# The gate/up accumulator tile U2 gets a second buffer

## The chip, the cores and the metric

The kernel runs on one core of a Trainium2 chip. The metric is device microseconds of one execution; the time before is the median of three runs. The profile is of one further execution, whose own time is given beside its span. TensorE (PE) multiplies; ScalarE (ACT), VectorE (DVE) and GpSimd (POOL) do the elementwise work; SyncE (SP) issues the DMAs.

## The reference

One layer of an encoder over x of 1024 rows and 1024 columns, in float32: a half-step feed-forward (FFN), an attention mixer of two head groups, a second half-step FFN. The change touches the FFNs alone:

```python
f = _swiglu(_rmsnorm(x, ffn1_pre_g[l]), ffn1_w_gate[l], ffn1_w_up[l], ffn1_w_down[l])
x = x + 0.5 * _rmsnorm(f, ffn1_post_g[l])
# _swiglu: (silu(x @ w_gate) * (x @ w_up)) @ w_down, with w_gate, w_up 1024 x 2816, w_down 2816 x 1024
```

## The kernel before

Each float32 operand of a matmul is split into a high and a low part, and three matmuls (high-high, high-low, low-high; PASSES) stand for one. The split of a weight tile is a ScalarE conversion (line 117) and a subtraction on GpSimd or VectorE (line 118), into a tile wgu of a pool of five.

The class Ffn runs each half-step. The 2816 hidden columns are cut into NF = 22 blocks of 128. Block 0 is done plainly. In blocks 1 to 21 (the loop over `self.items`, method `run`), the gate and up products of the block are done together by a seven-product scheme in the manner of Strassen and Winograd, in place of eight quarter products. Rows of activations are halved, the contraction is halved, and the 128 gate and 128 up columns are taken 64 at a time. Each product is 12 matmuls of 128x128 by 512 columns. Their order in a block is P1, P6, P2, P7, P5, P4, P3 (ORDER); the last block has P1, P6, P7, P2, P4, P5, P3 (LAST).

The products go to four PSUM banks: P1 and P2 to pa, P6 to pb, P7 and P4 to pc, P5 and P3 to pd. P2 is added by TensorE onto P1 in pa. P1 alone is needed too: after P1, line 409 copies it out of pa on ScalarE into the SBUF tile U2. VectorE adds P6 to U2 (line 411), makes U3 = U2 + P7 (414) and adds P5 to it (417), makes C21 = U2 + P4 (423), and last adds P3 to U2 itself (426). The function `glu` turns two such sums into half of a hidden tile h: silu of the gate half on ScalarE (line 445), times the up half on VectorE (line 446). It runs after P2 (from pa), P5 (from U3), P4 (from C21) and P3 (from U2). So U2 of a block is read for the last time by the multiply of line 446 after P3, while P1 and P6 of the next block run. Each of U2, U3 and C21 has one buffer in the pool u. In the profile all of them are named U or C.

While a block is multiplied, the weights of the next are made. `feed` calls `prepare` for the tiles some products ahead: it loads raw gate and up columns (line 180; the tile rawgu has three buffers), combines them on GpSimd (lines 213, 214, 223, 225) and splits them. After odd blocks, `keep` stores the h tiles of a pair in DRAM for the down projection (line 333), makes three differences and a sum of them on VectorE one by one (line 337) and stores these (line 338).

The engines have one queue each and take their instructions in the order of that queue. The framework's planner sets the order before the run by planned times and by the order of the code; `issue_after` holds an instruction behind another. So an instruction may stand earlier or later on its engine than the code has it: in the rows below, a conversion of line 117 often stands ahead of a silu that the code has first. The framework also adds the waits: a tile with one buffer may be written again only once its last reader is done.

Of the kernel before, what the change touches and what calls it, by code (L numbers as in the profile page):

```python
# [10 lines left out]
F32 = mybir.dt.float32  # L11
# [25 lines left out]
def tile_macaron_block(ctx, tc, x, f1_pre, f1_post, f1_g, f1_u, f1_d, mix_pre, mix_post, w_qkv,  # L37
# [13 lines left out]
    def open_pool(name, **kw):  # L51
        kw.setdefault("bufs", 1)
        return tc.alloc_tile_pool(name=name, reuse_waits="tile", **kw)
# [66 lines left out]
    class Ffn:  # L120
# [273 lines left out]

        def gate_up(self, i, prod, ps, y, psd):
            def U(name):
                return self.u.tile([128, 4, 128], F32, name=name)

            tt, add, s = DVE.tensor_tensor, OP.add, self.S
            n = (self.ORDER if i < NF - 1 else self.LAST).index(prod)  # L400
            if i == 1 and 0 < n < 5:
                self.turn_combo(("T2", "T3", "T1", "T4")[n - 1], y, psd)
            p = self.bank(i, ps, self.BANK[prod])
            first = prod in ("P1", "P6", "P7", "P5")
            name = {"P1": "B11", "P6": "T2", "P7": "T3", "P5": "T1", "P2": "B21", "P4": "T4", "P3": "B22"}[prod]
            self.product(p, self.W[i, prod], name, first)
            if prod == "P1":
                s["u2"], s["c21"] = U("U2"), U("C21")
                ACT.activation(s["u2"], p, AF.Copy)  # L409
            elif prod == "P6":  # L410
                tt(s["u2"], s["u2"], p, op=add)
            elif prod == "P7":
                s["u3"] = U("U3")
                tt(s["u3"], s["u2"], p, op=add)
            elif prod == "P5":
                s["h1"] = self.new_h(i, 1)
                tt(s["u3"], s["u3"], p, op=add)  # L417
                self.glu(s["h1"][64:128], s["u3"], s["c21"])
            elif prod == "P2":
                s["h0"] = self.new_h(i, 0)  # L420
                self.glu(s["h0"][0:64], p, s["h0"])
            elif prod == "P4":
                tt(s["c21"], s["u2"], p, op=add)
                self.glu(s["h0"][64:128], s["c21"], s["h0"])
            elif prod == "P3":
                tt(s["u2"], s["u2"], p, op=add)
                self.glu(s["h1"][0:64], s["u2"], s["c21"])
            if i == NF - 1 and n == 3:
                self.close_tx(2)
                self.raw.release()  # L430
                self.load_left(self.AHEAD)
                self.open_down()
            if n == 6 and i % 2 == 1 and i < NF - 1:
                self.keep(i // 2)
            if n == 6 and i >= NF - 2:
                for half in range(2):
                    SP.dma_start(self.hd["h", i, half], self.H[i][half])
            if n == 6 and i == NF - 1:
                self.close_tx(1)
                self.u.release()  # L440
                self.us = open_pool("us" + self.tag, side=self.near)
                self.U = self.us.tile([128, 4, 512], F32, name="U")
# [694 lines left out]
```

## Time and profile before

| what | value |
|---|---|
| median of three runs | 2077.77 us (2077.45 to 2078.15) |
| the profiled execution | 2079.25 us, span 2077.5 us |
| PE busy | 1983.2 us (95%) |
| DVE, ACT, POOL busy | 1333.0, 1005.9, 1048.3 us |
| granted PE clock, mean | 0.990 of full speed |
| the copies of line 409 start | from 55.5 to 469.4 us (first half-step) and from 1410.8 to 1824.6 us (second) |

Times in the rows are microseconds from the start of the span unless marked ns. A row of the timeline gives the start, the busy time, the engine, the line, the operation, output and inputs with their sizes, how many instructions are merged (x), and in brackets the idle time of the engine before it and what ended it. SPq is SyncE's queue of DMA issues, PEld the loading of weights. A wait for several semaphores is put down to the one that came last by the profile.

### The profile page before, as it was taken

What the parts mean: (1) busy time and instruction counts of PE and PEld (TensorE: products, weight loads), DVE (VectorE), ACT (ScalarE), POOL (GpSimd) and SP (SyncE); (2) the same over time, 40 slices, a digit from 0 to 9 for tenths busy, and PEclk for the clock granted to TensorE, in tenths of its full rate; (3) what the DMA queues carried; (4) which work ended last, traced back from release to release, by engine and by line L of the source; (5) the groups of instructions that cost most, each with busy time, mean ns of one, the idle gap of its engine ahead of it and who ended that gap; (6) DMA issues with size and microseconds to landing.
All of it is one profiled execution on the core that took longest, in us unless ns stands there. A gap on an engine that the chain in (4) does not pass through costs nothing. (4 is left out here: it accounts for less than half of the span.)

```text
span 2077.5 us, 30443 instructions
## 1 busy us (share of the span) xinstructions
PE 1983.2 (95%) x10728; PEld 1676.4 (81%) x10728; DVE 1333.0 (64%) x2255; ACT 1005.9 (48%) x1892; POOL 1048.3 (50%) x894
## 2 busy tenths in 40 slices
PE   7999999999999799999999999999999999999996
PEld 6777777777888699998999998887777777778884
DVE  7545544547668855766999888356545444576688
ACT  5433333334444433436999999234333333344443
POOL 4555656565050614233777887315565655651504
PEclk9999999999999899999999999999999999999998
DMA  4232322326533543233040643222323232365434
GB/s 147 75 98 87 116 92 87 112 87 228 177 117 95 199 130 101 67 102 77 2 138 1 207 137 90 102 77 71 100 78 125 79 101 84 115 221 170 127 97 172
DMA packets 210681, 233.01 MB, mean 112 GB/s; under 512 B 21088, under 2 KB 147040, under 8 KB 210400
## 3 DMA queue, kind: packets, MB, share of 16 engines
q1 hardware_dynamic: 210528, 231.06, 35.3%
q8 instruction: 85, 1.39, 0.3%
q14 instruction: 68, 0.56, 0.1%
HBM read 164.95 MB, written 66.06 MB: 111 GB/s over the span
## 5 line engine op out<-in xcount | busy, mean ns | idle before, releaser
L118 POOL TENSOR_TENSOR wgu<-rawgu,wgu 128x512 fp32r<-128x512 f32 x216 | 306.8, 1428 | 385.4 <-ACT wgu L117 358.8
L117 ACT ACTIVATE wgu<-rawgu 128x512 fp32r<-128x512 f32 x302 | 181.7, 627 | 368.0 <-POOL rawgu L225 190.5
L288 PE MATMUL pa<-actT,wgu 128*128 128x512 f32 (+1 forms) x1080 | 270.4, 398 | 29.7 <-ACT U L409 28.8
L356 PE MATMUL pd<-wgu 128*128 128x512 f32 x1140 | 272.4, 390 | 3.5 <-DVE wgu L118 3.2
L288 PEld LDWEIGHTS pa<-actT,wgu 128*128 128x128 f32 x1080 | 198.6, 190 | 89.2 <-ACT U L409 44.5
L356 PEld LDWEIGHTS pd<-wgu 128*128 128x128 f32 x1140 | 213.0, 188 | 52.5 <-DVE wgu L118 6.7
L567 PE MATMUL pq<-wq,actT 128*128 128x256 f32 x1728 | 217.7, 284 | 0.7 <-ACT actT L107 0.7
L567 PEld LDWEIGHTS pq<-wq,actT 128*128 128x128 f32 x1728 | 208.9, 190 | 1.3 <-ACT actT L107 1.0
L117 ACT ACTIVATE wgu<-b 128x512 fp32r<-128x512 f32 x148 | 93.0, 631 | 204.7 <-PE pd L356 114.8
L118 DVE TENSOR_TENSOR wgu<-b,wgu 128x512 fp32r<-128x512 f32 x144 | 120.3, 837 | 103.8 <-ACT wgu L117 103.4
L767 POOL TENSOR_SCALAR P<-P,il 128x1024 f32<-128x1024 f32 (+1 forms) x128 | 130.6, 1020 | 64.3 <-DVE il L766 61.1
L446 DVE TENSOR_TENSOR h<-h,C 64x512 f32<-64x512 f32 x42 | 51.5, 1226 | 156.9 <-ACT h L445 156.9
L868 DVE TENSOR_TENSOR PT<-pt,PT 128x512 fp32r<-128x512 f32 (+1 forms) x256 | 146.2, 612 | 2.0 <-ACT PT L867 2.0
L288 PE MATMUL pd<-actT,wgu 128*128 128x512 f32 x552 | 136.2, 395 | 0.0
L288 PE MATMUL pc<-actT,wgu 128*128 128x512 f32 x552 | 136.0, 394 | 0.0
L867 ACT ACTIVATE PT<-pt 128x512 fp32r<-128x512 f32 (+1 forms) x256 | 125.4, 544 | 10.5 <-PE pt L864 7.1
L864 PE MATMUL pt<-identr,P 128*128 128x128 f32 x896 | 125.0, 275 | 1.7 <-ACT vst L702 1.1
L288 PEld LDWEIGHTS pd<-actT,wgu 128*128 128x128 f32 x552 | 103.3, 187 | 25.7 <-DVE U L417 0.6
L288 PEld LDWEIGHTS pc<-actT,wgu 128*128 128x128 f32 x552 | 103.3, 187 | 25.0 <-DVE actT L108 0.4
L288 PE MATMUL pb<-tx,wgu 128*128 128x512 f32 x504 | 122.3, 391 | 0.0
L288 PE MATMUL pc<-tx,wgu 128*128 128x512 f32 x504 | 122.3, 391 | 0.0
L288 PE MATMUL pd<-tx,wgu 128*128 128x512 f32 x504 | 121.3, 389 | 0.0
(190 smaller groups left out, 3898.9 us busy)
## 6 DMA issues: line engine op xcount, KB each, us to landing
hd<-h SPq DMA_DIRECT2D x140, 256.0 KB, 2.9
h<-hd SPq DMA_DIRECT2D x140, 256.0 KB, 2.9
rawgu<-in_ffn_w_gate_dram SPq DMA_DIRECT2D x88, 256.0 KB, 3.0
rawgu<-in_ffn_w_up_dram SPq DMA_DIRECT2D x88, 256.0 KB, 3.7
b<-in_ffn_w_down_dram SPq DMA_DIRECT2D x88, 256.0 KB, 3.4
bkT<-kd SPq DMA_DIRECT2D x32, 320.0 KB, 7.3
rawq<-in_w_qkv_dram SPq DMA_DIRECT2D x16, 512.0 KB, 4.7
bV<-vd SPq DMA_DIRECT2D x8, 640.0 KB, 4.4
```

The costliest lines, as they stand in the source:

```text
L117: ACT.activation(hi, raw, AF.Copy)
L118: return eng.tensor_tensor(lo, raw, f32(hi), op=OP.subtract).ins
L288: PE.matmul(p[:, c0:c1, :], w[:, a, k, :], self.rhs(name, b, k)[:, c0:c1, :], start=(first and n == 0), stop=(n == 11), skip_group_check=True)
L356: PE.matmul(p, A[:, a, 128 * i:128 * i + 128], B[:, b, :], start=(first and start and n == 0), stop=(end and n == 2), skip_group_check=True)
L446: DVE.tensor_tensor(dst, s[64:128], c[64:128], op=OP.mult)
L567: PE.matmul(p, actT[:, a, T, k, :], WQ[j][:, b, k, :], start=(n == 0), stop=(n == 23))
L767: POOL.tensor_scalar(P[:, 0:w], P[:, 0:w], il, 1.0, op0=OP.mult, op1=OP.mult)
L864: PE.transpose(out=p[:, j, :], in_=col(P, b0 + j), identity=ident)
L867: ACT.activation(hv, p[:, 0:n, :], AF.Copy)
L868: DVE.tensor_tensor(lv, p[:, 0:n, :], f32(hv), op=OP.subtract)
```

## The change

The inner function U of `gate_up` makes the tiles U2, C21 and U3. U2 gets two buffers, so that those of successive blocks lie in different places; C21 and U3 keep one. The pool grows by 2 KB in each partition.

```diff
         def gate_up(self, i, prod, ps, y, psd):
             def U(name):
-                return self.u.tile([128, 4, 128], F32, name=name)
+                return self.u.tile([128, 4, 128], F32, name=name, bufs=2 if name == "U2" else 1)
```

## Rows read from the trace of the kernel before

**Rows 1.** The page: TensorE's busy time, share of the span, instructions

```profile
PE 1983.2 (95%) x10728; PEld 1676.4 (81%) x10728; DVE 1333.0 (64%) x2255; ACT 1005.9 (48%) x1892; POOL 1048.3 (50%) x894
```

**Rows 2.** Waits of PE, 105.2-451.5 and 1459.9-1807: us in all, times, longest

```profile
PE pa L288 <- ACT U L409: 12.7, 18, 1.0
...
PE pa L288 <- ACT U L409: 12.3, 18, 0.7
```

**Rows 3.** The timeline of one block: TensorE's products, and one load of weights

```profile
105.39 2.62 PEld L288 LDWEIGHTS pa<-actT,wgu 128*128 128x128 f32 x12 [1.10 <-ACT U L409]
105.40 3.06 PE L288 MATMUL pa<-actT,wgu 128*128 128x512 f32 x12 [0.68 <-ACT U L409]
108.29 2.90 PE L288 MATMUL pc<-tx,wgu 128*128 128x512 f32 x12
111.02 2.88 PE L288 MATMUL pd<-tx,wgu 128*128 128x512 f32 x12
...
119.33 2.96 PE L288 MATMUL pa<-actT,wgu 128*128 128x512 f32 x12
122.14 2.90 PE L288 MATMUL pb<-tx,wgu 128*128 128x512 f32 x12
125.72 2.59 PE L288 MATMUL pa<-actT,wgu 128*128 128x512 f32 x10 [0.69 <-ACT U L409]
```

**Rows 4.** The timeline of the same block: the other engines, from P2 on

```profile
108.49 0.59 ACT L445 ACTIVATE h<-pa 64x512 f32<-64x512 f32 x1 [2.11 <-PE pa L288]
...
111.06 1.29 POOL L213 TENSOR_TENSOR rawgu<-rawgu 128x512 f32<-128x512 f32 x1
...
113.75 1.16 ACT L117 ACTIVATE wgu<-rawgu 128x512 fp32r<-128x512 f32 x2 [4.02 <-POOL rawgu L214]
...
120.25 0.63 ACT L117 ACTIVATE wgu<-rawgu 128x512 fp32r<-128x512 f32 x1 [4.69 <-POOL rawgu L225]
120.91 0.63 ACT L445 ACTIVATE h<-C 64x512 f32<-64x512 f32 x1
120.96 1.30 POOL L118 TENSOR_TENSOR wgu<-rawgu,wgu 128x512 fp32r<-128x512 f32 x1 [0.74 <-ACT wgu L117]
...
121.58 1.23 DVE L446 TENSOR_TENSOR h<-h,C 64x512 f32<-64x512 f32 x1 [4.15 <-ACT h L445]
...
122.84 0.69 DVE L426 TENSOR_TENSOR U<-U,pd 128x512 f32<-128x512 f32 x1
...
123.62 0.63 ACT L445 ACTIVATE C<-U 64x512 f32<-64x512 f32 x1 [1.42 <-DVE U L426]
...
124.29 0.69 DVE L446 TENSOR_TENSOR h<-C,U 64x512 f32<-64x512 f32 x1 [0.16 <-ACT C L445]
...
125.07 0.60 ACT L409 ACTIVATE U<-pa 128x512 f32<-128x512 f32 x1 [0.81 <-PE pb L288]
125.56 1.14 ACT L117 ACTIVATE wgu<-rawgu 128x512 fp32r<-128x512 f32 x2
```

**Rows 5.** The timeline just after, where a pair of h tiles is stored

```profile
125.01 3.12 DVE L337 TENSOR_TENSOR h<-h 128x512 f32<-128x512 f32 x3
...
126.12 0.45 SPq L180 DMA_DIRECT2D rawgu<-in_ffn_w_up_dram  x1
126.26 1.31 POOL L118 TENSOR_TENSOR wgu<-rawgu,wgu 128x512 fp32r<-128x512 f32 x1 [4.00 <-ACT wgu L117]
```

**Rows 6.** The page's DMA issues: KB each, median us from issue to landing

```profile
rawgu<-in_ffn_w_up_dram SPq DMA_DIRECT2D x88, 256.0 KB, 3.7
```

**Rows 7.** The timeline around the copy of block 2

```profile
83.80 1.54 PE L288 MATMUL pb<-tx,wgu 128*128 128x512 f32 x6
...
84.16 0.60 ACT L409 ACTIVATE U<-pa 128x512 f32<-128x512 f32 x1 [0.81 <-DVE h L446]
```

**Rows 8.** Line 409: what ended ScalarE's idle time before it (us, times)

```profile
  PE pb L288: 28.5, 35
  DVE h L446: 4.1, 5
```

## The prediction

> **What bounds the kernel now.** The page comes first: TensorE is busy 1983.2 of the 2077.5 us [rows 1], so a change that touches no matmul can win only where TensorE stands still. The waits of TensorE come next, over the two stretches in which the gate/up blocks 3 to 20 of either half-step run: there it waits for one thing alone, the copy of U2 out of pa on line 409, 18 times in each stretch and 12.7 + 12.3 = 25.0 us in all, 0.69 us a block [rows 2]. The product behind the copy is P2: it adds into the bank pa that holds P1, so it may not start before the copy has read pa.
>
> Then one block is read in order of time. From the start of one P2 to that of the next: 125.72 - 105.40 = 20.32 us [rows 3]. TensorE alone would need less. P7, P5, P4, P3 and the next P1 take 122.14 - 108.29 = 13.85; P6, with nothing to wait for, takes what the first P7 took, 111.02 - 108.29 = 2.73; a P2 that doesn't restart takes what P1 took, 122.14 - 119.33 = 2.81. Sum 19.39 us. So 0.93 us a block is lost to the copy: 0.69 of idleness, some 0.16 by which TensorE stands before it shows as idle, and 0.08 because P2 after a stop took 108.29 - 105.40 = 2.89.
>
> Why is the copy late? Follow it back [rows 4]. P2 ends, ScalarE takes silu of it (108.49), then its conversions release GpSimd (111.06), GpSimd releases ScalarE (113.75, idle 4.02 until then), GpSimd's two combinations end, the conversion at 120.25 waits 4.69 for the last of them, silu of P4 is queued behind it (120.91), VectorE multiplies (121.58), adds P3 to U2 (122.84), ScalarE takes silu (123.62), VectorE multiplies (124.29), ScalarE copies (125.07), the next P2 starts (125.72). Each waits for the one before it, from one P2 to the next. This ring, 20.32 us long, sets the period; TensorE with its 19.39 does not.
>
> **The change.** It removes one link of the ring. The multiply at 124.29 reads the old U2; with one buffer the copy may not write the new one before it is done. The copy starts 125.07 - 124.29 = 0.78 us after the multiply starts. With a second buffer it no longer needs it: P1 has ended (P6 started at 122.14, behind it), and the buffer it then gets was last read one block, some 20 us, earlier. What is left ahead of the copy is the queue of ScalarE: the silu at 123.62 stands directly before it and lasts to 124.25. So the copy starts at 124.25 plus the gap between two ScalarE instructions. No row has this pair without a wait between. Bounds: the pair of conversions at 125.56 started 0.11 before the copy ended at 125.67; the conversion at 120.25 ended at 120.88, and the silu followed 0.03 later; the copy now starts 0.09 after the multiply has ended. From -0.11 to +0.09, then; I take 0.03, another ScalarE pair on SBUF. The copy starts at 124.28 or so, 0.78 to 0.79 earlier than now; by the bounds 0.73 to 0.93.
>
> What is late next: the copy, 0.60 long, ends at 124.88, P2 starts 0.05 behind it as now (125.72 after 125.67), at 124.93. TensorE alone would be ready at 122.14 + 2.73 = 124.87. So the ring still sets the period, by a hair: 20.32 - 0.78 = 19.54 us against 19.39 of TensorE. More than 0.93 a block can't be won however early the copy is.
>
> What else moves: ScalarE's two conversions behind the copy (125.56) and GpSimd's subtraction behind them (126.26) [rows 5] come 0.78 earlier; the weights they make are used some products later. VectorE's add of P6 into U2 follows the copy, but P6 itself ends only at about 125.0, so it starts then or, after pair blocks, behind the three h differences. The second buffer costs 2 KB a partition and no instruction. No matmul, DMA, or queue position is asked for by the diff. Blocks 1, 2 and 21 win nothing: in block 2 the copy was at 84.16 while P6 was still running from 83.80 on, and P2 followed without a wait [rows 7]; in block 21 P7 stands between P6 and P2. After the half-step all work follows, shifted, as it depends on it.
>
> Sum: 36 blocks x 0.78 = 28.1 us; by the bounds 36 x 0.73 = 26.3 to 36 x 0.93 = 33.5. The profiled execution took 2079.25 us (span 2077.5): 2051.2 after. The median of the runs, 2077.77, is 1.5 below the profiled one, and the gain is the same for both: **2049.7 us**.
>
> [...] In the rows the weight load of P2 waits for the copy with the matmul (105.39, idle 1.10 against 0.68 of the matmul), and P2 then takes 2.89 instead of 2.81. [...]
>
> **Rivals.**
> A, TensorE's own time becomes the period. The planner, free of the old wait, could put the copy ahead of the silu of P3, or the gap could be at its lower bound. P1 has ended by 119.33 + 2.96 = 122.29, and ScalarE stands idle for 1.42 before the silu at 123.62, so there is room. Then 36 x 0.93 = 33.5: 2044.3. Against: in the rows the planner lets the silu go first.
>
> B, the raw weights become the wait. In half of the blocks (those after a pair of h tiles is stored) the load of the up half is issued late, at 126.12, behind the store of the first h difference, which VectorE makes from 125.01 on [rows 5]. It lands 3.7 later (the median) [rows 6], at 129.8; GpSimd first needs it one period after 111.06, at 131.4: 1.6 us of slack, 0.8 after the change. That holds unless the first difference is delayed. GpSimd's subtraction moves from 126.26 to 125.48, still 0.47 behind that difference. The three differences take 3.12 together, over 1 us each, where GpSimd works beside them; and the multiply at 121.58, beside GpSimd at 120.96, took 1.23 where its like at 124.29 took 0.69. [...]
>
> C, slower: the planner places the copy behind the two conversions that now follow it. The second of them writes a weight slot that P6 must have left, so it waits to about 125.1 and lasts 0.57; the copy would start at 125.72, P2 at 126.37, 0.65 later than now: 36 x 0.65 = 23.4, 2101. The turning point: behind one conversion only, the copy starts at about 124.9 and the change still wins 0.19 a block (2071); behind both it loses. Against: the copy stands before them in the code, and both it and the first conversion are released by the end of P1.
>
> D, nothing happens: the wait view names TensorE's pb, not VectorE, as what ended 28.5 of ScalarE's idle time before the copy, 35 times, and VectorE's multiply only 5 times, 4.1 [rows 8]. Were it P6 that holds the copy, the second buffer would do nothing: 2077.8. But in block 2 the copy started after the same idle time (0.81) with P6 still running, put down to the multiply [rows 7]. P6 merely ends last by chance, in the few hundredths between; the view names what came last.
>
> **How the numbers follow.** Forecast 0.78 (2044.3 to 2051.5 by its bounds), A 0.08, B 0.06, and behind one conversion 0.02; C 0.03, D 0.03. The range 2043 to 2057 holds the forecast with its bounds, the rule on weight loads, and A; B to D stay out, with slips of a few us for loads that land late. A difference of 0.2% (4.2 us) is about what can be told from no change. Faster: 0.78 + 0.08 + 0.06 + 0.02 = 0.94; same: D, 0.03; slower: C, 0.03.
>
> **What would show it.** Right: P2 to P2 falls to about 19.54 us in blocks 3 to 20; the copy starts within 0.1 us of the end of the silu on C and before the multiply's end; TensorE's wait for it falls from 25.0 us to under 3; TensorE's busy time stays. A: 19.4 and no wait. B: alternate blocks at 19.5 and 20.3, with GpSimd's line 213 ended by a DMA. C: conversions between silu and copy. The prediction is wrong if the period stays at 20.3, or if another engine takes TensorE's wait.

## The result and the profile after

The changed kernel takes 2056.06 us (median of four runs, 2053.57 to 2057.92), the kernel before 2077.96 in the runs beside it: a ratio of 0.9897, 95% interval 0.9884 to 0.9909. It is 21.9 us faster. The forecast was 28.1 us faster, 2049.7 us; the range, 2043 to 2057, holds the time, near its upper end; the forecast's own bounds, 2044.3 to 2051.5, do not hold it.

The page of the changed kernel, part 1 (busy us, share of the span of 2055.0 us, instructions):

```profile
PE 1980.3 (96%) x10728; PEld 1676.8 (82%) x10728; DVE 1336.7 (65%) x2255; ACT 1005.9 (49%) x1892; POOL 1055.5 (51%) x894
```

TensorE is as busy as it was [rows 1], to 3 us; what shrank by 22.5 is the span. Every engine's queue holds the same instructions in the same order in both kernels, so whatever differs is waiting, or instructions that got slower. GpSimd is one such: 1055.5 us where it was 1048.3, with no instruction more.

TensorE's waits in the changed kernel, 100 to 440 us and 1445 to 1785 us (us in all, times, longest):

```profile
PE pa L288 <- ACT U L409: 2.4, 8, 0.3
...
PE pa L288 <- ACT U L409: 2.4, 8, 0.3
```

Where it stood 18 times in each half-step for 0.69 us [rows 2], it now shows a wait 8 times, of 0.3. A block in two still waits. The reason is seen in two blocks in a row. The timeline of the changed kernel, a block that ends with P2 at 122.05 and the next, which ends with P2 at 142.01:

```profile
101.88 0.60 ACT L409 ACTIVATE U<-pa 128x512 f32<-128x512 f32 x1
101.88 0.69 DVE L446 TENSOR_TENSOR h<-C,U 64x512 f32<-64x512 f32 x1 [0.15 <-ACT C L445]
...
102.53 2.62 PEld L288 LDWEIGHTS pa<-actT,wgu 128*128 128x128 f32 x12 [0.31 <-ACT U L409]
102.53 3.05 PE L288 MATMUL pa<-actT,wgu 128*128 128x512 f32 x12
...
105.41 2.93 PE L288 MATMUL pc<-tx,wgu 128*128 128x512 f32 x12
...
106.93 1.29 POOL L118 TENSOR_TENSOR wgu<-rawgu,wgu 128x512 fp32r<-128x512 f32 x1 [2.57 <-ACT wgu L117]
...
108.19 1.29 POOL L213 TENSOR_TENSOR rawgu<-rawgu 128x512 f32<-128x512 f32 x1
...
110.87 1.15 ACT L117 ACTIVATE wgu<-rawgu 128x512 fp32r<-128x512 f32 x2 [4.02 <-POOL rawgu L214]
...
120.74 0.63 ACT L445 ACTIVATE C<-U 64x512 f32<-64x512 f32 x1 [1.42 <-DVE U L426]
...
121.40 0.60 ACT L409 ACTIVATE U<-pa 128x512 f32<-128x512 f32 x1
121.40 0.69 DVE L446 TENSOR_TENSOR h<-C,U 64x512 f32<-64x512 f32 x1 [0.16 <-ACT C L445]
...
122.05 3.05 PE L288 MATMUL pa<-actT,wgu 128*128 128x512 f32 x12
...
122.13 3.12 DVE L337 TENSOR_TENSOR h<-h 128x512 f32<-128x512 f32 x3
122.59 1.38 POOL L118 TENSOR_TENSOR wgu<-rawgu,wgu 128x512 fp32r<-128x512 f32 x1 [3.21 <-ACT wgu L117]
...
126.36 0.69 DVE L337 TENSOR_TENSOR h<-h 128x512 f32<-128x512 f32 x1
126.46 1.74 POOL L118 TENSOR_TENSOR wgu<-rawgu,wgu 128x512 fp32r<-128x512 f32 x1 [2.49 <-ACT wgu L117]
...
128.16 1.29 POOL L213 TENSOR_TENSOR rawgu<-rawgu 128x512 f32<-128x512 f32 x1
...
130.84 1.15 ACT L117 ACTIVATE wgu<-rawgu 128x512 fp32r<-128x512 f32 x2 [4.46 <-POOL rawgu L214]
...
142.01 3.05 PE L288 MATMUL pa<-actT,wgu 128*128 128x512 f32 x12 [0.30 <-ACT U L409]
```

Read first the copy (line 409): it starts 0.66 behind the start of the silu, 0.03 behind its end, beside the multiply and no longer after it [rows 4]. Then from P2 to P2: 122.05 - 102.53 = 19.52 us, and 142.01 - 122.05 = 19.96. They alternate so through both half-steps: eight blocks in each take 19.96 to 19.99, the others 19.52 to 19.56 (the first, 19.43 and 19.45). The long block differs in one link of the ring: GpSimd's subtraction for the weights of P1 takes 1.74 where it takes 1.29 in the short one, and what follows is late by that (4.46 of waiting for 4.02). It started at 126.46 while VectorE had begun, at 126.36, the fourth operation on h of the stored pair (line 337; the three at 122.13 are the others). In the kernel before, the two just missed each other. Its timeline, the same place:

```profile
129.25 0.68 DVE L337 TENSOR_TENSOR h<-h 128x512 f32<-128x512 f32 x1
...
130.14 1.29 POOL L118 TENSOR_TENSOR wgu<-rawgu,wgu 128x512 fp32r<-128x512 f32 x1 [2.56 <-ACT wgu L117]
```

There the operation had ended at 129.93, 0.21 before GpSimd began. The change moved the ring, and this subtraction with it, some 0.8 us ahead of VectorE's queue, into that operation.

### The profile page after: what moved, and what is told of

Its sections match the earlier page's. It is cut to its first block, busy times and chain, and to the rows that moved or that the text cites. A ratio compares the mean times of both kernels' runs of the same rounds, so it can differ in the third digit from the quotient of the medians.

```text
span 2055.0 us, 30441 instructions
## 1 busy us (share of the span) xinstructions
PE 1980.3 (96%) x10728; PEld 1676.8 (82%) x10728; DVE 1336.7 (65%) x2255; ACT 1005.9 (49%) x1892; POOL 1055.5 (51%) x894
## 5 line engine op out<-in xcount | busy, mean ns | idle before, releaser
L118 POOL TENSOR_TENSOR wgu<-rawgu,wgu 128x512 fp32r<-128x512 f32 x216 | 315.5, 1469 | 354.3 <-ACT wgu L117 332.2
```

Source lines behind the costliest of these rows:

```text
L118: return eng.tensor_tensor(lo, raw, f32(hi), op=OP.subtract).ins
```

## The experiments

Theory 1: VectorE's fourth operation, with two inputs in SBUF, holds GpSimd's subtraction off. Theory 2, from rival B: the raw weights of those blocks land too late. Theory 3: VectorE's queue is too full there. Each ratio below is to the kernel before, run beside: 2076.34 us with the first four runs, 2077.6 with the last four.

**The changed kernel again**, as base for the next three on the same chip.

> The changed kernel once more, beside the others on one chip, as their base. All theories: about 2056 us, blocks of 19.5 and 19.96 us in turn, GpSimd's subtraction for P1 (line 118, after P2's silu) 1.74 us long where a stored pair's fourth difference runs on VectorE, 1.29 elsewhere.

2056.55 us, ratio 0.9903 (0.9885 to 0.9920); 19.52 to 19.57 and 19.94 to 20.02 us in turn, the subtraction 1.74 to 1.76 and 1.29.

**The fourth operation a block later.** It goes to a list of its own, which is emptied at P2 of the next odd block, and is held there behind VectorE's add of P6.

```diff
-                    DVE.tensor_tensor(o, p, q, op=op)
+                    with tc.issue_after(self.p6) if k == 6 else ExitStack(): DVE.tensor_tensor(o, p, q, op=op)
...
-                self.late.append(made)
+                (self.last4 if k == 6 else self.late).append(made)
...
-                tt(s["u2"], s["u2"], p, op=add)
+                self.p6 = tt(s["u2"], s["u2"], p, op=add).ins
...
-                self.add_late(1)
+                self.add_late(1, it[0] == "D" or it[2] == "P2" and it[1] % 2 == 1)
```

> The changed kernel with the fourth of a pair's operations on h (line 337, k = 6) made one block later, behind VectorE's add of P6 there, when GpSimd is idle. Theory 1 (that operation, with two SBUF inputs, holds GpSimd's subtraction for P1 off, a link of the ring, for 0.45 us in 16 blocks): all blocks 19.52, that subtraction 1.29 everywhere, 16 x 0.44 = 7 us less, 2049 us. Theory 2 (the raw load of a stored pair's block lands too late): the load of up columns keeps its place behind the first difference, so 19.96 in turn and 2056. Theory 3 (VectorE's queue is too full in those blocks): the operation now fills the other blocks, which lose 0.4 in their place: about 2056, with the long and the short blocks exchanged.

2050.53 us, ratio 0.9869 (0.9852 to 0.9886). Its timeline, GpSimd's subtraction in the block of a stored pair, and the operation in the next:

```profile
126.86 1.29 POOL L118 TENSOR_TENSOR wgu<-rawgu,wgu 128x512 fp32r<-128x512 f32 x1 [2.51 <-ACT wgu L117]
...
144.28 0.68 DVE L337 TENSOR_TENSOR h<-h 128x512 f32<-128x512 f32 x1
...
146.39 1.29 POOL L118 TENSOR_TENSOR wgu<-rawgu,wgu 128x512 fp32r<-128x512 f32 x1 [2.58 <-ACT wgu L117]
```

The operation lies where GpSimd is idle, the subtraction takes 1.29 on both sides, and the blocks take 19.52 to 19.57 (one took 19.66; the first of each half-step, 19.44 and 19.45). Theory 1 foretold this. Theory 2 falls, as the up load kept its place (issued 1.11 behind the start of the first operation in both kernels, at 123.62 here and at 123.24 in the changed kernel), and theory 3, as the other blocks did not become long.

**The fourth operation at its old place, with one input in PSUM.**

```diff
-                    DVE.tensor_tensor(o, p, q, op=op)
+                    DVE.tensor_tensor(o, p, q if k < 6 else self.P[2 * j + 2, "b"].rearrange("p t f -> p (t f)"), op=op)
```

> The changed kernel with the fourth operation at its old place and of its old size, but its second input read from the PSUM bank pb and not from SBUF (so the hidden tile of that operation is wrong: part of the down projection's input is replaced). Theory 1 (two SBUF inputs hold GpSimd off): GpSimd's subtraction for P1 falls from 1.74 to 1.29, all blocks 19.52, 2049 us. Theory 2 (raw load) and theory 3 (VectorE's queue): nothing changes, 19.96 in turn, 2056 us.

2049.49 us, ratio 0.9867 (0.9852 to 0.9882), blocks of 19.52 to 19.58 (the first, 19.43 and 19.45). Its timeline:

```profile
128.48 0.68 DVE L337 TENSOR_TENSOR h<-h,pb 128x512 f32<-128x512 f32 x1
...
128.58 1.29 POOL L118 TENSOR_TENSOR wgu<-rawgu,wgu 128x512 fp32r<-128x512 f32 x1 [2.49 <-ACT wgu L117]
```

The two start 0.10 apart, as in the changed kernel, and run beside each other; the subtraction takes 1.29 where it took 1.74. So it is not that VectorE is busy, but where this operation reads: with its second input in PSUM instead of SBUF, the 0.45 is gone.

**One buffer for U2, but the sum with P3 goes to U3** (from the kernel before).

```diff
-                tt(s["u2"], s["u2"], p, op=add)
-                self.glu(s["h1"][0:64], s["u2"], s["c21"])
+                tt(s["u3"], s["u2"], p, op=add)
+                self.glu(s["h1"][0:64], s["u3"], s["c21"])
```

> The kernel before, with one buffer for U2 as it was, but the sum with P3 (line 426) written to U3 in place of U2, so that the multiply after P3 no longer reads U2. If the wait of the copy for that multiply is what the second buffer removed, this removes it too, with no memory: copy straight behind the silu, blocks 19.5 and 19.96 in turn, 2056 us. If the gain came from the place or the size of the pool, or from a new order, nothing: 2078 us.

2056.05 us, ratio 0.9901 (0.9884 to 0.9919), blocks of 19.52 to 19.57 and 19.95 to 20.02 in turn, subtraction 1.74 to 1.76 in the long ones. The same gain and the same loss with no memory: what the second buffer took away is the copy's wait for the multiply, and nothing else that shows.

The next four test the ring as a whole. In it the silu of P4 stands behind a conversion that waits for GpSimd (4.69 at 120.25 [rows 4]), though it needs nothing of GpSimd's.

**That conversion held behind the silu of P4**, in the changed kernel.

```diff
-            ACT.activation(s[64:128], c[0:64], AF.Silu)
+            self.silu = ACT.activation(s[64:128], c[0:64], AF.Silu).ins
...
-            return split(hi, lo, src, eng)
+            with tc.issue_after(self.silu) if key[1] == "P7" and 1 < key[0] < NF - 1 else ExitStack(): return split(hi, lo, src, eng)
```

> The changed kernel with the conversion of the next block's P7 weights (line 117, the one that waits 4.7 us for GpSimd) held behind the silu of P4 on ScalarE. If the ring through that conversion sets the period (my theory), the ring is cut: silu of P4 no longer waits for GpSimd, the copy comes as soon as P1 ends, and TensorE's own 19.39 us is the period in all 36 blocks, whether VectorE holds GpSimd off or not: 2077.9 - 36 x 0.95 = 2044 us, no wait of TensorE for the copy. Rival (each block is held by the raw loads, or by VectorE): 2056, as without it.

2044.17 us, ratio 0.9840 (0.9827 to 0.9853); every one of the 36 blocks 19.37 (first half-step) or 19.40 (second), and TensorE waits for no copy.

**The same edit in the kernel before**, with one buffer.

> The kernel before, U2 with one buffer, with that same conversion held behind the silu of P4. If the ring is the cause and the single buffer only its last link, the multiply after P3 is done before P1 ends and the single buffer costs nothing: 19.39 us a block, 2044 us, better than the second buffer alone. Rival (the single buffer by itself costs 0.78 a block, wherever the silu stands): about 2072, and not under 2056.

2044.35 us, ratio 0.9841 (0.9827 to 0.9854), the same block times. Its timeline:

```profile
95.67 0.63 ACT L445 ACTIVATE h<-C 64x512 f32<-64x512 f32 x1 [1.95 <-DVE C L423]
...
98.74 1.15 ACT L117 ACTIVATE wgu<-rawgu 128x512 fp32r<-128x512 f32 x2 [2.44 <-POOL rawgu L225]
...
100.29 2.90 PE L288 MATMUL pb<-tx,wgu 128*128 128x512 f32 x12
101.33 0.69 DVE L446 TENSOR_TENSOR h<-C,U 64x512 f32<-64x512 f32 x1
102.11 0.60 ACT L409 ACTIVATE U<-pa 128x512 f32<-128x512 f32 x1 [1.56 <-DVE h L446]
...
102.80 2.74 PEld L288 LDWEIGHTS pa<-actT,wgu 128*128 128x128 f32 x12
103.02 2.96 PE L288 MATMUL pa<-actT,wgu 128*128 128x512 f32 x12
...
105.81 2.90 PE L288 MATMUL pc<-tx,wgu 128*128 128x512 f32 x12
```

The silu of P4 runs 3 us ahead of the conversion. The copy still waits for the multiply of line 446, 0.78 from start to start as ever, but ends at 102.71, before TensorE is through with P6 (100.29 + 2.90 = 103.19) and before the next load of weights starts (102.80): the wait is there and costs nothing. That load goes 0.22 ahead of its matmul again.

**Both edits**: the conversion held, the fourth operation moved.

> The changed kernel with both: the conversion held behind the silu of P4, and the fourth operation one block later. Ring theory: nothing is left to win by the second, 2044 us as with the conversion alone. [...]

2044.47 us, ratio 0.9844 (0.9831 to 0.9858); blocks 19.37 and 19.40. The second edit wins nothing here. That alone does not show that the longer subtraction is free once the ring is cut, for in the changed kernel with the conversion alone held the two had ceased to meet:

```profile
127.29 0.68 DVE L337 TENSOR_TENSOR h<-h 128x512 f32<-128x512 f32 x1
...
128.35 1.29 POOL L118 TENSOR_TENSOR wgu<-rawgu,wgu 128x512 fp32r<-128x512 f32 x1 [4.17 <-ACT wgu L117]
```

The operation ended 0.38 before GpSimd began. But GpSimd and VectorE are busy for longer there than in the changed kernel (1064.9 and 1352.3 us, against 1055.5 and 1336.7) with the same instructions, and TensorE shows no wait: what slows those two engines there costs nothing that shows.

**The fourth operation moved in the kernel before**, alone.

> The kernel before with the fourth operation one block later and nothing else. If that operation met GpSimd's subtraction only because the change moved the ring 0.78 us ahead of it, nothing is to be won here: 2077 us, 20.33 in all blocks. If it cost 0.44 in half of the blocks already before, 2070.

2078.85 us, ratio 1.0006 (0.9997 to 1.0015); blocks of 20.3 as before. Nothing to be won there: the subtraction of 1.74 for P1 came with the change.

## Why the prediction was right, and where it was off

*The ring, and the link taken out of it*: right, as shown by the sum with P3 in U3. Without the collision a block takes 19.52 us, against 19.54 foretold; the copy starts 0.03 behind the silu, the value taken. Without anything else 36 blocks would have won 0.81 each, 29 us; the two runs without the collision were 25.8 and 26.9 us under the kernel before beside them. The sign of a wait under 3 us failed: 2.4 + 2.4 = 4.8, all in the long blocks.

*TensorE's own time, 19.39 us*: right to 0.02, as shown where the ring is cut. Rival A's time fits too: 2044.3 foretold, 2044.17 measured, though by another edit than the one it named.

*What else moves*: this step failed. It took the first three of VectorE's four operations on a stored pair (it calls them three differences; they are a sum and two differences) and left the fourth out; and it said of GpSimd only that one subtraction (126.26 [rows 5]), off the ring, comes earlier. The subtraction for P1, on the ring, comes earlier too, and meets the fourth operation: 0.44 us in 16 blocks, 7.0 us. 29 - 7 = 22; 21.9 was measured, 19.8 in the repeat. That the range held the time is luck: for what lies between the forecast's bounds and 2057 the prediction names nothing but slips of loads that land late, and no load was the cause.

*Rival B* came near the cause and weighed it at the wrong place: it took VectorE's longer times beside GpSimd (1.23 at 121.58, 0.69 at 124.29 [rows 4]) for what could delay a load, and did not ask whether GpSimd's times grow beside VectorE (1.74 for 1.29). Its sign "alternate blocks" came, at 19.52 and 19.96 instead of 19.5 and 20.3, but line 213 is not ended by a DMA; the raw loads hold nothing.

*Rival D*: wrong, as argued. The copy's wait was put down to P6, and it fell with the multiply.

*Weight loads*: the row held in the changed kernel (P2 took 105.41 - 102.53 = 2.88, for 2.89 [rows 3]), since the copy still ended too late for the load, which waited 0.31 for it and started with its matmul, at 102.53. Where the copy ends early, as in the kernel before with the conversion held, the load runs 0.22 ahead of its matmul and P2 takes 105.81 - 103.02 = 2.79. The range counts in a rule on weight loads that no run shows: in these two blocks the load started after the copy had ended, 0.05 (102.53 after 102.48) and 0.09 (102.80 after 102.71) behind it.

*Rival C* did not arise: the queues kept their order.

## What to carry to other kernels

The wait that lay in a ring of dependencies gave back its own length here (0.78 foretold, 0.81 found where no collision came in), and a second buffer is one way of several to remove it; here the same came free by writing the last sum to another tile, and more came from the order of two instructions on one engine. Follow the ring to the link that waits for something it does not need: there it is cut. And when a ring moves against a queue that stays, go over every pair of instructions on it and beside it of which one takes longer beside the other (here 1.74 us for 1.29), not only those that the change names.

## What was not expected

Two kernels that differ in no instruction's place can differ in the length of one: GpSimd's subtraction for P1 took 1.74 us where it began 0.10 behind the start of VectorE's fourth operation, with both inputs in SBUF, and 1.29 where it began 0.21 behind its end.

The price stood in the trace of the kernel before, where it could have been read. Block after block there, the multiply after P5, with both inputs in SBUF, begins just ahead of another subtraction of GpSimd, which takes 1.75; in every second block the multiply after P2, with one input in the bank pa, begins 0.18 or more ahead of the one for P1 and still runs when that begins, and that takes 1.29:

```profile
129.96 0.69 DVE L446 TENSOR_TENSOR h<-h,pa 64x512 f32<-64x512 f32 x1
130.14 1.29 POOL L118 TENSOR_TENSOR wgu<-rawgu,wgu 128x512 fp32r<-128x512 f32 x1 [2.56 <-ACT wgu L117]
...
135.94 0.71 DVE L446 TENSOR_TENSOR h<-C,U 64x512 f32<-64x512 f32 x1 [0.99 <-ACT C L445]
...
136.05 1.75 POOL L118 TENSOR_TENSOR wgu<-rawgu,wgu 128x512 fp32r<-128x512 f32 x1
```
